# S5 on one core: the second family of outer products as swapped, negated copies

## The chip, the cores and the metric

The kernel runs on one core of a Trainium2 chip. The metric is the device time of one execution in microseconds; the median of several runs counts. Engines are named as in the profile: PE (TensorE), DVE (VectorE), ACT (ScalarE), POOL (GpSimd) and SP (the queue that issues DMAs). PEld is PE's loading of weights.

## What is computed

The kernel computes a whole network block and a second, two-layer one on 1024 tokens of width 1024, in float32. The change lies in one branch of the first block, the S5 state-space layer. It has 32 groups of 16 channels, and each group drives a complex diagonal state of 64 numbers:

```
bu_re = jnp.einsum('gpc,btgc->btgp', bbar_re, uf)
bu_im = jnp.einsum('gpc,btgc->btgp', bbar_im, uf)
_, _, x_re, x_im = lax.associative_scan(_complex_linear_combine, (a_re, a_im, bu_re, bu_im), axis=1)
y = (jnp.einsum('gcp,btgp->btgc', c_re.astype(f32), x_re)
     - jnp.einsum('gcp,btgp->btgc', c_im.astype(f32), x_im))
y = y.reshape(bsz, t, S5_WIDTH) + d_skip.astype(f32) * u.astype(f32)
```

Beside S5 stand a gated linear attention (GLA), an mLSTM, projections with gates and a feed-forward network; then the second block with a latent attention, a memory attention and a linear recurrence.

## The kernel before

Large matrix products are made of three matmuls each (`mm3`, L130): operands are split into a high and a low part (wh and wl of weights, ah and al of activations). Almost all work of DVE and POOL goes through small helpers, so a profile row names the helper's line: L136 is a two-operand operation, L145 a scalar-tensor-tensor, L142 a tensor-scalar, L148 an activation, L120 a matmul, L127 a transpose on PE.

S5 is done in chunks of 8 time steps, so that 1024 steps become 128 chunks. `s5_pre` (L636) makes tables once: E1 and E2 (powers of the diagonal state matrix times cosine and minus sine, in the lower 64 partitions a quarter turn further), the B and C matrices with sign, and the phases. `s5_core` (L734) runs eight times, for four groups each (hb 0 to 7); one such pass is called a round here. A round

- makes co and si, cosines and sines of the chunks' phases (x, y on DVE, two Sin activations and a square on ACT, `cossin` L725);
- makes outer products of B or C with powers (`prod`, L753): W1 on DVE; M1, M2 and W2 on POOL. M1 and W1 are one family; M2 and W2 are what they become when the state is multiplied by i. Each is a sum of two products, and each product is one instruction per group: 128x144 on DVE, 128x128 on POOL;
- transposes M1 and M2 on PE into a PSUM tile each and copies them to V1 and V2 with ACT (L772);
- multiplies the B columns (s_bst) with W1 into the kernel K of a chunk (L777 on), copies it with ACT (L779) and spreads it by eight DMAs into Tm (L783), to which DVE adds the skip weight on the diagonal (L785);
- loads the inputs U by eight DMAs, multiplies V1 and V2 with them into pa and pb (PSUM), turns those with co and si into va and vb, adds them, scans along the chunks (four scans, L808), and turns back into va and vb;
- adds Tm x U, W1 x va and W2 x vb in PSUM, and evicts that with a Gelu on ACT into ys, which a DMA stores.

va and vb share their buffers with x and y, so the next round's x waits until PE has read va.

The rounds are coroutines. Between them the main program goes on with large projections (four tiles `in_gqk`, one `in_misc`, then `in_v`, eight results of 24 matmuls each, evicted as e by ACT at L544). A planner mixes them: it keeps a clock (`self.clk`) that each matmul and transpose advances (L119, L126), and a coroutine that yields 14.0, 9.0 or 7.0 is resumed when the clock has gone on that far. Within what this emits, the framework's scheduler orders the instructions of each engine when the program is built; on the chip every engine works its queue in that fixed order. PSUM tiles for small results come from two rings, of three buffers and of one (`psc`, L233); every fourth call takes the second.

```
prod(W1, self.s5cr, self.s5E1, self.s5ci, self.s5E2, 0, 9, ALU.add, nc.vector, "tm")
prod(M1, self.s5br, self.s5E1, self.s5bi, self.s5E2, 9, 8, ALU.add, nc.gpsimd, "tmp")
prod(M2, self.s5bi, self.s5E1, self.s5br, self.s5E2, 9, 8, ALU.subtract, nc.gpsimd, "tmp")
prod(W2, self.s5cr, self.s5E2, self.s5ci, self.s5E1, 1, 8, ALU.subtract, nc.gpsimd, "tmp")
```

Of the kernel before, what the change touches and what calls it, by code (L numbers as in the profile page):

```python
# [10 lines left out]
F32 = mybir.dt.float32  # L11
# [3 lines left out]
AF = mybir.ActivationFunctionType  # L15
ALU = mybir.AluOpType
# [35 lines left out]
class Kernel:  # L52
# [681 lines left out]
    def s5_core(self, hb, pm, pu, pt, su, turn):  # L734

        nc = self.nc
        g0 = 4 * hb
        gs = slice(g0, g0 + 4)
        if hb:
            yield from self.join(turn[hb - 1])  # L740
        co = pm.tile([128, 4, 129], F32, tag="co", name="co")
        si = pm.tile([128, 4, 129], F32, tag="si", name="si")
        x = pt.tile([128, 4, 129], F32, tag="x", name="x")
        y = pt.tile([128, 4, 129], F32, tag="y", name="y")
        self.tt(x, self.s5ph[:, gs].unsqueeze(2).to_broadcast([128, 4, 129]),
                self.s5k[:, 17:146].unsqueeze(1).to_broadcast([128, 4, 129]), ALU.mult)
        self.cossin(co, si, x, y)
        W1 = pm.tile([128, 4, 9, 16], F32, tag="W1", name="W1")
        W2 = pm.tile([128, 4, 8, 16], F32, tag="W2", name="W2")
        M1 = pt.tile([128, 4, 8, 16], F32, tag="M1", name="M1")  # L750
        M2 = pt.tile([128, 4, 8, 16], F32, tag="M2", name="M2")

        def prod(out, m1, e1, m2, e2, a, n, op, eng, tag):  # L753
            tm = pt.tile([128, 4, 9, 16], F32, tag=tag, name="tm")
            for g in range(4):
                Eg = lambda e: e[:, g0 + g, a:a + n].unsqueeze(2).to_broadcast([128, n, 16])
                Cg = lambda m: m[:, g0 + g].unsqueeze(1).to_broadcast([128, n, 16])
                self.tt(tm[:, g, 0:n], Cg(m1), Eg(e1), ALU.mult, eng=eng)
                self.tt(out[:, g], Cg(m2), Eg(e2), ALU.mult, eng=eng)
            self.tt(out, tm[:, :, 0:n], out, op, eng=eng)  # L760
        prod(W1, self.s5cr, self.s5E1, self.s5ci, self.s5E2, 0, 9, ALU.add, nc.vector, "tm")
        prod(M1, self.s5br, self.s5E1, self.s5bi, self.s5E2, 9, 8, ALU.add, nc.gpsimd, "tmp")
        prod(M2, self.s5bi, self.s5E1, self.s5br, self.s5E2, 9, 8, ALU.subtract, nc.gpsimd, "tmp")
        prod(W2, self.s5cr, self.s5E2, self.s5ci, self.s5E1, 1, 8, ALU.subtract, nc.gpsimd, "tmp")
        yield 14.0
        V1 = pm.tile([128, 4, 128], F32, tag="V1", name="V1")
        V2 = pm.tile([128, 4, 128], F32, tag="V2", name="V2")
        for M, V in ((M1, V1), (M2, V2)):
            ps = self.psc()
            for g in range(4):  # L770
                self.tr(ps[:, g * 128:g * 128 + 128], M[:, g].rearrange("p a b -> p (a b)"))
            nc.scalar.copy(V, ps.rearrange("p (g n) -> p g n", g=4))  # L772
        self.finish(turn[hb])
        K = pt.tile([16, 4, 128], F32, tag="K", name="K")
        ps = self.psc()
        for g in range(4):
            self.mm(ps[0:16, g * 128:g * 128 + 128], self.s5bst[:, g0 + g],  # L777
                    W1[:, g, 0:8].rearrange("p a b -> p (a b)"), True, True)
        nc.scalar.copy(K, ps[0:16].rearrange("p (g n) -> p g n", g=4))  # L779
        Tm = pm.tile([128, 4, 128], F32, tag="Tm", name="Tm")  # L780
        nc.gpsimd.memset(Tm, 0.0)
        for j in range(8):
            nc.sync.dma_start(Tm[16 * j:16 * j + 16, :, 16 * j:128], K[:, :, 0:128 - 16 * j])  # L783
        for g in range(4):
            self.stt(Tm[:, g], self.ident, self.s5d[:, g0 + g:g0 + g + 1], Tm[:, g], ALU.mult, ALU.add)  # L785

        yield from self.join(su[hb // 2])
        U = pu.tile([128, 4, 128], F32, tag="U", name="U")
        src = self.d_u[hb // 2].rearrange("(g c) (j n) -> j c g n", g=8, j=8)
        for j in range(8):  # L790
            nc.sync.dma_start(U[16 * j:16 * j + 16], src[j][:, 4 * (hb % 2):4 * (hb % 2) + 4])
        Z = pu.tile([128, 4, 129], F32, tag="Z", name="Z")
        nc.gpsimd.memset(Z[:, :, 0:1], 0.0)
        yield 9.0
        va = pt.tile([128, 4, 128], F32, tag="x", name="va")
        vb = pt.tile([128, 4, 128], F32, tag="y", name="vb")
        pa, pb = self.psc(), self.psc()
        r4 = lambda a: a.rearrange("p (g n) -> p g n", g=4)
        for g in range(4):
            c = slice(g * 128, g * 128 + 128)  # L800
            self.mm(pa[:, c], V1[:, g], U[:, g], True, True)
            self.mm(pb[:, c], V2[:, g], U[:, g], True, True)
        self.tt(va, r4(pa), co[:, :, 1:129], ALU.mult)
        self.tt(vb, r4(pb), si[:, :, 1:129], ALU.mult)
        self.tt(va, va, vb, ALU.add)
        for g in range(4):
            R = self.s5R[:, g0 + g:g0 + g + 1].to_broadcast([128, 128])
            nc.vector.tensor_tensor_scan(out=Z[:, g, 1:129], data0=R, data1=va[:, g], initial=0.0,  # L808
                                         op0=ALU.mult, op1=ALU.add)
        self.tt(va, Z[:, :, 0:128], co[:, :, 0:128], ALU.mult)  # L810
        self.tt(vb, Z[:, :, 0:128], si[:, :, 0:128], ALU.mult)
        yield 7.0
        ys = pt.tile([128, 4, 128], F32, tag="ys", name="ys")
        ps = self.psc()
        for g in range(4):
            c = slice(g * 128, g * 128 + 128)
            self.mm(ps[:, c], Tm[:, g], U[:, g], True, False)
            self.mm(ps[:, c], W1[:, g, 1:9].rearrange("p a b -> p (a b)"), va[:, g], False, False)
            self.mm(ps[:, c], W2[:, g].rearrange("p a b -> p (a b)"), vb[:, g], False, True)
        self.act(ys, r4(ps), AF.Gelu_apprx_tanh)  # L820
        nc.sync.dma_start(self.d_sy[hb // 2][:, 512 * (hb % 2):512 * (hb % 2) + 512], ys.rearrange("p g n -> p (g n)"))
# [1071 lines left out]
    def mla_attn(self, d_mem):  # L1893

        nc, A = self.nc, self.A
        with ExitStack() as es:
# [164 lines left out]
            def take(gen, n):  # L2061
                for _ in range(n):
                    next(gen, None)
# [11 lines left out]
            M0 = (0, 0, 0, 0, 6, 1, 1, 1, 1, 0, 0, 0)  # L2075
            M1 = (0, 0, 0, 0, 0, 0, 1, 4, 2, 3, 4, 2)
            steps = []
# [6 lines left out]
            for n, (u, kb, first, last) in enumerate(steps):  # L2084
# [9 lines left out]
                take(mx[0], (M0[i] + 1) // 2)  # L2094
                take(mx[1], (M1[i] + 1) // 2)
                while len(pend) > 2 or (pend and n == len(steps) - 1):
# [9 lines left out]
                take(mx[0], M0[i] // 2)  # L2106
                take(mx[1], M1[i] // 2)
                take(pj, PJ[i])
# [379 lines left out]
```

## Time and profile before

| | us |
|---|---|
| median of 3 runs | 2833.54 (2833.21 to 2842.47) |
| the profiled execution | 2830.67 |
| its span, first to last instruction | 2828.9 |
| busy in the span: PE, DVE, ACT, POOL | 2681.6, 1719.8, 931.4, 858.8 |
| mean granted clock of PE | 0.978 of full speed |

The profile is of one execution. Busy time is the time in which an engine works on at least one instruction; matmuls overlap, so their starts tell their pace better than their durations. A window's row gives, for a stretch of the span, the busy time of each engine with its instructions, and the clock that PE was granted (1.00 is 2.4 GHz, 0.50 would be 1.2 GHz throughout). A wait's row says which operation stood idle until which other operation ended.

### The profile page before, as it was taken

How to read it: one execution, taken by the hardware profiler on the slowest of the kernel's cores; microseconds unless marked ns; L12 is line 12 of the kernel's file. 1: busy time of each engine (PE TensorE's matmuls, PEld its weight loads, DVE VectorE, ACT ScalarE, POOL GpSimd, SP SyncE). 2: the span in 40 equal slices, each digit the busy share in tenths (PEclk: the TensorE clock that was granted, in tenths of full speed). 3: DMA queues.
4: the chain of work that ended last, by engine and by line, in shares of the span. 5: the costliest groups of instructions: out<-in, count | busy, mean ns of one | idle time of the engine just before them, and what ended most of it. 6: DMA issues, size and time to landing. Idle time of an engine off the chain costs nothing. (4 is left out here: it accounts for less than half of the span.)

```text
span 2828.9 us, 40596 instructions
## 1 busy us (share of the span) xinstructions
PE 2681.6 (95%) x16104; PEld 2210.0 (78%) x16104; DVE 1719.8 (61%) x2467; ACT 931.4 (33%) x1431; POOL 858.8 (30%) x771
## 2 busy tenths in 40 slices
PE   6989899899999999799999999999989998999998
PEld 5769688688878899689898888787766665976688
DVE  7896975662643245944444466653577777667586
ACT  6453544311111133422222321242333434146330
POOL 4694561000000003744444200141213547013332
PEclk8999999999999999899999999999999999999999
DMA  8323224552645242222222423342220113322231
GB/s 245 109 74 111 98 79 139 171 185 98 234 176 168 75 164 97 76 86 79 90 71 86 149 90 103 107 144 90 81 82 29 34 44 106 141 82 61 74 110 62
DMA packets 133917, 304.13 MB, mean 108 GB/s; under 512 B 18032, under 2 KB 61888, under 8 KB 133600
## 3 DMA queue, kind: packets, MB, share of 16 engines
q1 hardware_dynamic: 133728, 301.54, 31.6%
q8 instruction: 127, 2.08, 0.3%
q14 instruction: 62, 0.51, 0.1%
HBM read 226.20 MB, written 73.94 MB: 106 GB/s over the span
## 5 line engine op out<-in xcount | busy, mean ns | idle before, releaser
L120 PE MATMUL psg<-ah,wh 128*128 128x512 f32 x1392 | 560.4, 404 | 11.4 <-ACT ah L424 7.5
L120 PE MATMUL psg<-ah,wl 128*128 128x512 f32 x1392 | 554.8, 399 | 3.0 <-DVE wl L136 3.0
L120 PE MATMUL psg<-al,wh 128*128 128x512 f32 x1392 | 553.7, 398 | 1.8 <-DVE al L136 1.7
L136 DVE TENSOR_TENSOR wl<-wr,wh 128x1024 fp32r<-128x1024 f32 (+3 forms) x212 | 274.3, 1296 | 374.2 <-ACT wh L179 252.4
L179 ACT CAST wh<-wr 128x1024 fp32r<-128x1024 f32 (+3 forms) x161 | 162.3, 1010 | 775.5 <-PE psg L120 352.8
L120 PEld LDWEIGHTS psg<-ah,wh 128*128 128x128 f32 x1392 | 263.6, 190 | 79.2 <-issue 11.0
L120 PEld LDWEIGHTS psg<-al,wh 128*128 128x128 f32 x1392 | 264.5, 190 | 65.7 <-issue 5.3
L120 PEld LDWEIGHTS psg<-ah,wl 128*128 128x128 f32 x1392 | 264.3, 190 | 64.4 <-DVE wl L136 3.9
L120 PE MATMUL psc<-wh,ah 128*128 128x256 f32 x1024 | 290.5, 284 | 8.4 <-DVE ystore L136 4.3
L120 PE MATMUL psc<-wl,ah 128*128 128x256 f32 x1024 | 287.2, 281 | 0.0
L120 PE MATMUL psc<-wh,al 128*128 128x256 f32 x1024 | 286.5, 281 | 0.0
L142 POOL TENSOR_SCALAR rsv<-ss 128x1 f32<-128x1 f32 x32 | 11.3, 354 | 754.0 <-DVE ss L1249 512.1
L120 PEld LDWEIGHTS psc<-wh,ah 128*128 128x128 f32 x1024 | 196.6, 192 | 13.3 <-DVE ystore L136 5.0
L120 PE MATMUL psc<-tx,wh 128*128 128x256 f32 x1088 | 195.1, 280 | 2.6 <-DVE e L136 2.6
L120 PEld LDWEIGHTS psc<-wl,ah 128*128 128x128 f32 x1024 | 195.8, 191 | 0.3
L120 PEld LDWEIGHTS psc<-wh,al 128*128 128x128 f32 x1024 | 195.4, 191 | 0.1
L136 POOL TENSOR_TENSOR e<-e 128x1024 f32<-128x1024 f32 (+3 forms) x65 | 109.4, 1687 | 242.7 <-ACT e L148 122.9
L120 PEld LDWEIGHTS psc<-tx,wh 128*128 128x128 f32 x1088 | 169.3, 188 | 6.0 <-issue 2.8
L136 POOL TENSOR_TENSOR acc<-acc,e 128x512 f32<-128x512 f32 (+2 forms) x60 | 116.2, 1937 | 158.9 <-PE psc L120 156.5
L136 DVE TENSOR_TENSOR e<-psc,e 128x512 f32<-128x512 f32 (+1 forms) x138 | 89.8, 666 | 106.5 <-PE psc L120 106.4
L120 PE MATMUL psc<-tx,wl 128*128 128x256 f32 x544 | 152.1, 280 | 0.0
L120 PE MATMUL psc<-wh,gh 128*128 128x512 f32 x352 | 139.1, 397 | 2.4 <-ACT gh L1470 2.4
(488 smaller groups left out, 5454.4 us busy)
## 6 DMA issues: line engine op xcount, KB each, us to landing
wr<-in_w_ws_dram SPq DMA_DIRECT2D x45, 512.0 KB
wr<-in_ffn_in_dram SPq DMA_DIRECT2D x44, 512.0 KB
aw<-in_ada_w_dram SPq DMA_DIRECT2D x32, 512.0 KB
wr<-in_w_out_dram SPq DMA_DIRECT2D x24, 512.0 KB
d_h<-e SPq DMA_DIRECT2D x22, 512.0 KB
wr<-in_ffn_out_dram SPq DMA_DIRECT2D x22, 512.0 KB
e<-d_h SPq DMA_DIRECT2D x22, 512.0 KB
e<-d_y SPq DMA_DIRECT2D x20, 512.0 KB
```

The costliest lines, as they stand in the source:

```text
L120: self.nc.tensor.matmul(out, lhsT, rhs, start=start, stop=stop)
L136: (eng or self.nc.vector).tensor_tensor(out=out, in0=a, in1=b, op=op)
L142: (eng or self.nc.vector).tensor_scalar(out=out, in0=a, scalar1=s1, scalar2=s2, op0=op0, op1=op1)
L179: (self.nc.vector.tensor_copy if self.hi_dve else self.nc.scalar.copy)(hi[:, :n], raw[:, :n])
```

## The change

The families are no longer computed twice. Because the lower 64 partitions of E1 and E2 are a quarter turn ahead, the second family is the first with its halves of 64 swapped, one of them negated. W2 is made by two ACT copies from W1, one of each half, the second with scale -1. M2 is not made at all: M (formerly M1) is transposed once, and V2 comes from the same PSUM tile as V1, by two ACT copies of 64 columns per group each. The products that remain (W1 on DVE, M on POOL) run over four groups in one instruction.

```diff
@@ -747,29 +747,32 @@
         W1 = pm.tile([128, 4, 9, 16], F32, tag="W1", name="W1")
         W2 = pm.tile([128, 4, 8, 16], F32, tag="W2", name="W2")
-        M1 = pt.tile([128, 4, 8, 16], F32, tag="M1", name="M1")
-        M2 = pt.tile([128, 4, 8, 16], F32, tag="M2", name="M2")
-
-        def prod(out, m1, e1, m2, e2, a, n, op, eng, tag):
-            tm = pt.tile([128, 4, 9, 16], F32, tag=tag, name="tm")
-            for g in range(4):
-                Eg = lambda e: e[:, g0 + g, a:a + n].unsqueeze(2).to_broadcast([128, n, 16])
-                Cg = lambda m: m[:, g0 + g].unsqueeze(1).to_broadcast([128, n, 16])
-                self.tt(tm[:, g, 0:n], Cg(m1), Eg(e1), ALU.mult, eng=eng)
-                self.tt(out[:, g], Cg(m2), Eg(e2), ALU.mult, eng=eng)
-            self.tt(out, tm[:, :, 0:n], out, op, eng=eng)
-        prod(W1, self.s5cr, self.s5E1, self.s5ci, self.s5E2, 0, 9, ALU.add, nc.vector, "tm")
-        prod(M1, self.s5br, self.s5E1, self.s5bi, self.s5E2, 9, 8, ALU.add, nc.gpsimd, "tmp")
-        prod(M2, self.s5bi, self.s5E1, self.s5br, self.s5E2, 9, 8, ALU.subtract, nc.gpsimd, "tmp")
-        prod(W2, self.s5cr, self.s5E2, self.s5ci, self.s5E1, 1, 8, ALU.subtract, nc.gpsimd, "tmp")
+        M = pt.tile([128, 4, 8, 16], F32, tag="M", name="M")
+
+        def prod(out, m1, m2, a, n, eng, tag):
+
+            tm = pt.tile([128, 4, 9, 16], F32, tag=tag, name="tm")[:, :, 0:n]
+            Eg = lambda e: e[:, gs, a:a + n].unsqueeze(3).to_broadcast([128, 4, n, 16])
+            Cg = lambda m: m[:, gs].unsqueeze(2).to_broadcast([128, 4, n, 16])
+            self.tt(tm, Cg(m1), Eg(self.s5E1), ALU.mult, eng=eng)
+            self.tt(out, Cg(m2), Eg(self.s5E2), ALU.mult, eng=eng)
+            self.tt(out, tm, out, ALU.add, eng=eng)
+        prod(W1, self.s5cr, self.s5ci, 0, 9, nc.vector, "tm")
+        prod(M, self.s5br, self.s5bi, 9, 8, nc.gpsimd, "tmp")
+
+        top, bot = slice(0, 64), slice(64, 128)
+        nc.scalar.copy(W2[top], W1[bot, :, 1:9])
+        self.act(W2[bot], W1[top, :, 1:9], AF.Copy, scale=-1.0)
         yield 14.0
         V1 = pm.tile([128, 4, 128], F32, tag="V1", name="V1")
         V2 = pm.tile([128, 4, 128], F32, tag="V2", name="V2")
-        for M, V in ((M1, V1), (M2, V2)):
-            ps = self.psc()
-            for g in range(4):
-                self.tr(ps[:, g * 128:g * 128 + 128], M[:, g].rearrange("p a b -> p (a b)"))
-            nc.scalar.copy(V, ps.rearrange("p (g n) -> p g n", g=4))
+        ps = self.psc()
+        for g in range(4):
+            self.tr(ps[:, g * 128:g * 128 + 128], M[:, g].rearrange("p a b -> p (a b)"))
+        pv = ps.rearrange("p (g n) -> p g n", g=4)
+        nc.scalar.copy(V1, pv)
+        nc.scalar.copy(V2[:, :, top], pv[:, :, bot])
+        self.act(V2[:, :, bot], pv[:, :, top], AF.Copy, scale=-1.0)
         self.finish(turn[hb])
```

A round calls `psc` five times instead of six, and the planner's clock gets four transposes less a round, so the queues of S5 are ordered anew; behind S5 only the first GLA steps stand otherwise than before. On PE, the distance between a round's products with U and its output products is 30 to 35 large matmuls in the rounds 2 to 4, as before; the transposes and the product for K of the next round lie in it, after 12 of them. In the rounds beside `in_v`, three results of 24 lie in it instead of two.

POOL's queue before, one round of four groups (W_ and M_ with numbers are that round's W2, M1 and M2):

```order
L136 TENSOR_TENSOR M_1675<-s_bi,s_E_866 128x128 x4
L136 TENSOR_TENSOR tm<-s_br,s_E_865 128x128 x4
L136 TENSOR_TENSOR M_1676<-s_br,s_E_866 128x128 x4
L793 MEMSET Z 128x4
L136 TENSOR_TENSOR M_1675<-tm,M_1675 128x512
L136 TENSOR_TENSOR tm<-s_bi,s_E_865 128x128 x4
L136 TENSOR_TENSOR M_1676<-tm,M_1676 128x512
L781 MEMSET Tm 128x512
L136 TENSOR_TENSOR W_1674<-s_m,s_E_865 128x128 x4
L136 TENSOR_TENSOR tm<-s_m,s_E_866 128x128 x4
L136 TENSOR_TENSOR W_1674<-tm,W_1674 128x512
```

and in the changed program:

```order
L796 MEMSET Z 128x4
L136 TENSOR_TENSOR tm<-s_br,s_E_865 128x4x128
L784 MEMSET Tm 128x512
L136 TENSOR_TENSOR M<-s_bi,s_E_866 128x512
L136 TENSOR_TENSOR M<-tm,M 128x512
```

Of 24 products and three sums, two products and one sum are left.

ACT's queue before, from one output of S5 (ys) to the next table load for an output (V_1616 and V_1617 are a round's V1 and V2):

```order
L148 ACTIVATE ys<-psc 128x512
L148 ACT_TABLE_LOAD
L148 ACTIVATE si<-x 128x516
L148 ACTIVATE co<-x 128x516
L148 ACTIVATE co<-co 128x516
L772 COPY V_1616<-psc 128x512
L772 COPY V_1617<-psc 128x512
L179 CAST wh<-wr 128x1024
L601 COPY e<-psg 128x1024
L779 COPY K<-psc 16x512
L148 ACT_TABLE_LOAD
```

and the same stretch now (W_1373 is W2, W_1372 is W1):

```order
L148 ACTIVATE ys<-psc 128x512
L764 COPY W_1373<-W_1372 64x512
L148 ACTIVATE W_1373<-W_1372 64x512
L148 ACT_TABLE_LOAD
L148 ACTIVATE si<-x 128x516
L148 ACTIVATE co<-x 128x516
L148 ACTIVATE co<-co 128x516
L773 COPY V_1480<-psc 128x512
L774 COPY V_1481<-psc 128x4x64
L148 ACTIVATE V_1481<-psc 128x4x64
L782 COPY K<-psc 16x512
```

The two W2 copies have come between ys and the table load for the sines, and V2 is two instructions.

DVE's queue now, from a round's x on (W_1533 is W1; before, the products with tm and W stood as four of 128x144, and the additions to Tm among those with tm):

```order
L136 TENSOR_TENSOR x<-s_ph,s_kr 128x516
L136 TENSOR_TENSOR W_1533<-s_m,s_E_866 128x576
L145 SCALAR_TENSOR_TENSOR Tm<-ident,s_d,Tm 128x128 x4
L142 TENSOR_SCALAR y<-x 128x516
L136 TENSOR_TENSOR W_1533<-tm,W_1533 128x576
L136 TENSOR_TENSOR x<-x,y 128x516
L136 TENSOR_TENSOR tm<-s_m,s_E_865 128x576
L136 TENSOR_TENSOR vb<-psc,si 128x512
L136 TENSOR_TENSOR va<-psc,co 128x512
L142 TENSOR_SCALAR co<-co 128x516
L136 TENSOR_TENSOR va<-va,vb 128x512
```

The additions to Tm have moved ahead in the round; in the first round they stand just before the last row shown, in the third before the first.

## Rows read from the trace of the kernel before

**Rows 1.** The page, part 1: busy us, share of the span, instructions.

```profile
PE 2681.6 (95%) x16104; PEld 2210.0 (78%) x16104; DVE 1719.8 (61%) x2467; ACT 931.4 (33%) x1431; POOL 858.8 (30%) x771
```

**Rows 2.** Windows: PE, PEld, DVE, ACT, POOL busy, PEclk, DMA share, GB/s.

```profile
110.00:150.00 40.00, 34.72 (x197) 27.45 (x196) 32.49 (x50) 17.75 (x25) 39.37 (x65) 1.00 0.27 87
150.00:190.00 40.00, 35.27 (x201) 29.23 (x202) 34.95 (x57) 16.90 (x22) 39.29 (x66) 0.96 0.26 77
190.00:230.00 40.00, 34.15 (x238) 30.49 (x237) 38.87 (x65) 20.26 (x27) 34.80 (x54) 0.87 0.29 95
230.00:280.00 50.00, 49.83 (x398) 47.10 (x397) 27.81 (x48) 18.39 (x29) 17.69 (x29) 0.97 0.31 93
```

**Rows 3.** Waits of PE, 110 to 235 us: total us, times, longest.

```profile
PE psc L120 <- DVE va L136: 4.5, 3, 2.2
PE psc L120 <- ACT V L772: 3.2, 1, 3.2
PE psc L127 <- ACT e L544: 2.0, 1, 2.0
PE psc L127 <- DVE va L136: 2.0, 2, 1.8
PE psc L120 <- ACT e L544: 2.0, 1, 2.0
```

**Rows 4.** Window of one round of S5, columns as in rows 2.

```profile
155.83:173.87 18.04, 16.54 (x99) 13.34 (x98) 16.94 (x27) 8.46 (x11) 17.80 (x29) 1.00 0.18 60
```

**Rows 5.** Tile tm and its readers: ns min/median/max, first and last start, forms.

```profile
L136 POOL TENSOR_TENSOR tm<-s_br,s_E x32: 399/461/1265, 98.9 to 224.9; 128x128 f32<-128x128 f32 x32
L136 DVE TENSOR_TENSOR tm<-s_m,s_E x32: 293/504/520, 99.3 to 228.1; 128x144 f32<-128x144 f32 x32
...
L136 DVE TENSOR_TENSOR W<-tm,W x8: 746/951/1742, 105.9 to 245.1; 128x576 f32<-128x576 f32 x8
L136 POOL TENSOR_TENSOR W<-tm,W x8: 1267/1285/2372, 117.9 to 243.7; 128x512 f32<-128x512 f32 x8
```

**Rows 6.** Timeline of DVE, POOL busy beside it and later idle: start, duration.

```profile
167.08 0.89 DVE L136 TENSOR_TENSOR va<-va,vb 128x512 f32<-128x512 f32 x1
168.00 1.94 DVE L808 TENSOR_TENSOR_SCAN Z<-s_R,va 128x128 f32<-128x128 f32 x4
...
250.26 0.69 DVE L136 TENSOR_TENSOR va<-va,vb 128x512 f32<-128x512 f32 x1
250.99 1.37 DVE L808 TENSOR_TENSOR_SCAN Z<-s_R,va 128x128 f32<-128x128 f32 x4
```

**Rows 7.** Timeline of PE: transposes of M1 and M2 together, and of one.

```profile
180.98 1.03 PE L127 MATMUL psc<-ident,M 128*128 128x128 f32 x8
...
203.84 0.60 PE L127 MATMUL psc<-ident,M 128*128 128x128 f32 x4
```

**Rows 8.** Groups of ACT, 76 to 285 us: count, busy us, mean ns, idle before.

```profile
L148 ACT ACT_TABLE_LOAD x19 | 24.4, 1283 | 4.4 <-DMA cum<-d_gc 4.1
...
L772 ACT COPY V<-psc 128x512 f32<-128x512 f32 x16 | 8.9, 582 | 4.9 <-PE psc L127 4.8
L544 ACT COPY e<-psc 128x256 f32<-128x256 f32 x16 | 5.8, 369 | 25.4 <-PE psc L120 25.4
```

**Rows 9.** Timeline of PE: two large matmuls in a row at full clock.

```profile
284.59 0.39 PE L120 MATMUL psg<-ah,wh 128*128 128x512 f32 x1
284.82 0.39 PE L120 MATMUL psg<-al,wh 128*128 128x512 f32 x1
```

**Rows 10.** Timeline: K's copy on ACT, and DVE's addition to that Tm.

```profile
251.42 0.58 ACT L779 COPY K<-psc 16x512 f32<-16x512 f32 x1 [0.39 <-PE psc L120]
...
259.27 1.14 DVE L145 SCALAR_TENSOR_TENSOR Tm<-ident,s_d,Tm 128x128 f32<-128x128 f32 x4 [5.59 <-DMA Tm<-K]
```

**Rows 11.** Timeline of DVE: x and tm of a round with POOL mostly idle.

```profile
223.83 0.83 DVE L136 TENSOR_TENSOR x<-s_ph,s_kr 128x516 f32<-128x516 f32 x1
...
227.48 0.95 DVE L136 TENSOR_TENSOR tm<-s_m,s_E 128x144 f32<-128x144 f32 x4
```

## The prediction

> **What bounds the kernel now.** The page's busy shares come first: PE is busy 95% of the span and DVE 61%, POOL 30% [rows 1], so a gain has to come out of PE's own work, out of the 5% in which it stands still, or out of stretches at the lower clock. Then the stages: S5 lies between about 100 and 280 us, and its windows show all three at once [rows 2]. In 110 to 230 PE is idle for 5.28 + 4.73 + 5.85 = 15.9 us (the next 50 us add 0.17). In the same 120 us POOL is busy 39.37, 39.29 and 34.80 of every 40 and DVE 32.5 to 38.9; after 230, when POOL's S5 work runs out, PE is full. The granted clock is 1.00, 0.96, 0.87 and 0.97 of full speed; shares below 1 are time at 1.2 instead of 2.4 GHz behind such idle stretches, and cost about 0.04 x 35.3 + 0.13 x 34.2 + 0.03 x 49.8 = 7.3 us of PE.
>
> Who ends PE's idle time stands in the waits of 110 to 235 [rows 3]: mostly va, DVE's last link, as operand or as the reader that frees a PSUM tile, then the V copies on ACT (once, at the start), and ACT's e copies (twice 2.0 us). So the stage is set by DVE with POOL beside it. A round of four groups, from one start of x to the next, is 18.04 us long [rows 4]; POOL is busy 17.8 of it, DVE 16.9, PE 16.5, ACT 8.5. Two engines are full, and the third waits a little for them.
>
> **What the change removes.** POOL: of a round's 24 outer products of 128x128 and three sums of 128x512, two products and one sum of 128x512 are left. The sum alone takes 1.27 us at least, 1.29 in the median [rows 5]; a product over four groups is at least that long and at most four small ones, 4 x 0.46 = 1.84. So POOL's S5 arithmetic falls from some 17 us a round to 3.8 to 5.0.
>
> DVE: eight products of 128x144 become two of 128x576. The small ones take 0.29 us at best and 0.50 in the median, the sum of 576 elements 0.75 and 0.95 [rows 5]; 8 x 0.50 = 4.0 against 2 x 0.95 = 1.9, or 2.3 against 1.5 without contention. I take 1.5 us a round.
>
> DVE's other instructions get shorter as well, because POOL leaves. The same add takes 0.89 us beside POOL and 0.69 without it, the four scans 1.94 and 1.37 [rows 6]. That is about a quarter of what they cost; on 16.9 us of DVE less the 1.5 just counted, that is some 3 to 4 us where POOL is away. DVE's round falls to about 11 to 12 us of work against PE's 16. It is then no longer full, and neither is POOL.
>
> PE: four of eight transposes a round go. Four take 0.60 us by themselves and eight 1.03 [rows 7], so four cost 0.43 and eight rounds 3.4 us. This is PE's own work and comes off the end whatever else happens.
>
> **What it adds.** ACT gets the two W2 copies of 64x512, and V2 as two halves of 128x256 where one copy of 128x512 stood. The nearest rows are 0.58 for a 128x512 copy and 0.37 for 128x256 [rows 8]; K's copy of 16x512 takes 0.58 [rows 10], so elements per partition count, and partitions don't. No row shows a copy that moves half the partitions to the other half: between 0.37, if half the volume were half the work, and the 1.28 of a table load, the dearest small thing on ACT, I take 0.6, by the two rows of 512 elements. The far end would add 1.4 us of latency a round. That makes 2 x 0.6 + 2 x 0.37 - 0.58 = 1.4 us a round, on an engine busy 8.5 of 18. As load it is free. As latency it is not: by the order the copies stand between ys and the next table load (1.28 us), so that load, done early before, now follows the W2 copies, which follow DVE's W1. Behind them wait si, co, the V copies and, in the last rounds, the e copies that free PE's PSUM tiles. Counted from the end of a round's output products, DVE makes x, y, W1 and x in 2.9 us (3.65 from x to tm in a round without POOL, less 0.7 for the four small products that become one) [rows 11], the W2 copies end at 3.5, the load at 4.8, si and both co steps at 6.6. DVE meets co in its queue between the products va, vb and their sum, which it reaches at about 5.8 (12 large matmuls and the eight products with U come first on PE). It waits 1 us there and ends va and vb at 10.2 to 11.2. PE needs va after 12 + 12 + 18 large matmuls at 0.23 us [rows 9] and some 3.1 us of small ones, at about 12.7. The cover is 1.5 to 2.5 us; it holds, and were it gone each microsecond would cost one per round.
>
> The order moves one more thing. The diagonal addition to Tm is now queued on DVE ahead of that sum in the first round, and at the head of the round in the third. Tm is ready 7.3 us after the copy of K ends [rows 10]. In the first round that puts va some 1 to 2 us after PE's arrival; in the third it delays x by under 2 us, inside the cover. The eight DMAs a round that carry K into Tm, the loads of U and the weight loads are the same in number.
>
> **The sum**, against the profiled execution's 2830.67 us (2.9 under the median of the three runs, 2833.54). Transposes: -3.4. Idle: of 15.9 us, the waits on DVE and V go; the two waits on ACT's e copies (4.0) need not, since they come in the long cumulative sums of the gate, and 1 us in the first round is new. I count -11. Clock: idle that goes takes its slow stretch with it, in proportion 11 / 15.9 of 7.3, rounded down to -4 because the deepest stretch, 0.87, is the one with the e copies. Outside S5 the two programs are ordered alike but for the early GLA steps, where rows change places within a few microseconds: 0, within -3 and +3. Together -18.4. On the median that is 2815.1, on the profiled execution 2812.3; I say **2814**. Its own range: at best every idle and slow microsecond comes back, 3.4 + 15.9 + 7.3 = 26.6, which is 2804 on the profiled execution.
>
> **Rival 1: latency instead of load.** PE's waits were those of one chain per round (co, va, vb, scan, va, vb), and the chain keeps its length: DVE's instructions get shorter, but the W2 copies and the exposed table load on ACT and the wait for Tm's DMA in DVE's queue put back what that saved. For it: ACT was idle half the round and yet PE waited once for its V copies. Against it: in rows 6 the chain shrinks by a fifth as soon as POOL stops, and from 230 on PE had no wait. PE then gains the transposes, the start-up wait of 3.2 and 1 to 2 us of clock, 8 us: 2825. From where: if the chain ends 2 us later than I add it up.
>
> **Rival 2, slower: the long POOL instruction shuts DVE out.** Four short instructions become one of 1.3 us or more, and M waits for the transposes, so POOL starts its block just when DVE is on the chain's sum, scans and products. If each of the three made DVE wait out its whole length, at worst the 2.3 us of the longest 512-element row [rows 5], the chain would grow by 6.9 us. Less 3 us for the cover and the shorter instructions, that is 3.9 us of idle a round, 31 in eight, where 16 are now; the slow clock would double with it. That gives +15 + 7 - 3.4 = +19, about 2852. It decides from 5 us a round on. Against it: sums of 512 elements already stand three times a round on POOL, and DVE beside them was lengthened by 0.2 us in the median of its own sum (0.75 to 0.95) and by 1.0 at most [rows 5]. The Trainium skill's "SBUF — State Buffer", section "Who interferes with whom", has the rule that speaks for it: a DVE instruction with two SBUF inputs and a POOL instruction that reads SBUF contend for a port pair that is locked for the whole instruction, and the later one blocks fully. By that rule in its strict form the 6.9 us hold and the time is rival 2's. The trace agrees that the two contend, but its 0.2 us beside a POOL sum of 1.29 us is far from a full block.
>
> That the work is not really removed is no rival: the order lists the two products and the sum on POOL, and four transposes.
>
> **Chances.** Forecast 0.66; rival 1 0.27; rival 2 0.05; another slow-down, in the reordered GLA steps, 0.02. About 0.5%, or 14 us, is what a measurement of this kernel can tell from no change, so "faster" means below 2819.4: the forecast and its best bound lie there. Rival 1 lies within 0.5%, rival 2 and the rest above. So 0.66, 0.27, 0.07. The range goes from the best bound, 2804, to rival 1 with the 3 us of the GLA steps, 2828.
>
> **What would show it.** Right: from 110 us on POOL busy under 8 us in 20 and PE's idle under 6 us up to the end of S5, rounds of 16 to 16.5 us, the scans of a round near 1.4 us, 32 transposes of M instead of 64, the last S5 output near 258 instead of 277 us, GLA as long as before. Rival 1: DVE idle on co or on Tm's DMA in each round, and PE waiting for va by 1 us or more. Rival 2: DVE products of 1.5 us and more beside POOL's. Wrong altogether: S5 ends 15 us or more earlier, and the stages behind it give that back.

## The result, and the profile after

The changed kernel takes 2812.11 us (median of 5 runs, 2806.06 to 2820.0), the kernel before 2833.54 (5 runs, 2829.37 to 2842.47): a ratio of 0.9921, 95% interval 0.9895 to 0.9948. The profiled execution of the changed kernel took 2806.06 us with a span of 2804.2; it is the fastest of the five, so its positions are compared with those of the profiled execution before, stage by stage, and not the two spans.

Page, part 1 (against [rows 1]), then the windows of S5 (against [rows 2]; columns as there). POOL has lost 100 us, DVE 32.5; PE's share is the same 95% of a shorter span.

```profile
PE 2671.5 (95%) x16072; PEld 2203.3 (79%) x16072; DVE 1687.3 (60%) x2419; ACT 940.9 (34%) x1455; POOL 758.6 (27%) x579
```

```profile
110.00:150.00 40.00, 38.94 (x224) 32.18 (x223) 27.66 (x52) 22.62 (x36) 9.23 (x11) 1.00 0.36 111
150.00:190.00 40.00, 40.00 (x235) 33.40 (x235) 31.21 (x51) 28.43 (x39) 9.04 (x10) 0.96 0.30 94
190.00:230.00 40.00, 37.34 (x301) 35.83 (x300) 30.55 (x58) 23.71 (x37) 9.87 (x10) 0.91 0.35 107
```

PE is idle for 1.06, 0 and 2.66 us of the three windows, where it was 5.28, 4.73 and 5.85; POOL went from 39, 39 and 35 of 40 to between 9 and 10. From one start of x to the next (131.73, 147.78, 161.84) two rounds take 16.1 and 14.1 us instead of 18.04 [rows 4]. The groups of ys, the output of a round, give the end of S5: its last start moves from 277.1 to 255.9 us. First the kernel before, then the changed one (ns min/median/max, first and last start).

```profile
L148 ACT ACTIVATE ys<-psc x8: 597/599/602, 135.3 to 277.1; 128x512 f32<-128x512 f32 x8
```

```profile
L148 ACT ACTIVATE ys<-psc x8: 597/598/600, 129.7 to 255.9; 128x512 f32<-128x512 f32 x8
```

The waits of PE from 100 to 300 us (against [rows 3]) have none left for va of S5 and none for e on ACT; the 2.7 for vb is one wait near 208 us, the 0.8 for V is S5's start, and the three others lie behind 262 us, at the beginning of GLA. One wait of 0.3 for W at the start is not shown.

```profile
PE psc L120 <- DVE e L145: 4.7, 1, 4.7
PE psc L120 <- DVE vb L136: 2.7, 1, 2.7
PE psc L120 <- ACT P L954: 2.3, 1, 2.3
PE psc L120 <- DVE mx L136: 2.1, 1, 2.1
PE psc L120 <- ACT V L773: 0.8, 1, 0.8
```

GLA then gives a part back. The windows go from 100 us to GLA's first d, on to its last Sz, and over both; first before, then changed.

```profile
100.00:281.70 181.70, 165.67 (x1082) 143.90 (x1081) 144.09 (x236) 75.65 (x105) 141.16 (x231) 0.95 0.29 91
281.70:428.60 146.90, 128.64 (x2314) 111.13 (x2313) 120.09 (x198) 71.82 (x171) 85.77 (x91) 0.93 0.26 92
100.00:428.60 328.60, 294.31 (x3394) 255.02 (x3393) 264.18 (x434) 147.47 (x276) 226.92 (x322) 0.94 0.28 91
```

```profile
100.00:260.10 160.10, 156.04 (x1043) 137.77 (x1042) 111.79 (x190) 86.60 (x131) 39.38 (x40) 0.97 0.33 103
260.10:410.10 150.00, 133.44 (x2321) 115.18 (x2320) 121.12 (x197) 71.82 (x171) 86.69 (x91) 0.89 0.26 90
100.00:410.10 310.10, 289.48 (x3362) 252.95 (x3361) 232.91 (x386) 158.42 (x301) 126.07 (x131) 0.93 0.29 97
```

Up to GLA 21.6 us are gained. GLA takes 3.1 longer for almost the same number of matmuls: its PE idle falls by 1.7 us, its PE time rises by 4.8 at a granted clock of 0.89 instead of 0.93. Over both, 18.5 us are gained, 13.7 of idle (34.3 to 20.6) and 4.8 of PE's busy time.

One thing stands in the new trace that the old one hid. The timelines of POOL and DVE from 99 us on, where POOL starts on M; the changed kernel:

```profile
99.06 1.48 POOL L136 TENSOR_TENSOR tm<-s_br,s_E 128x512 f32<-128x512 f32 x1 [19.89 <-DVE s_E L136]
100.50 1.58 POOL L136 TENSOR_TENSOR M<-s_bi,s_E 128x512 f32<-128x512 f32 x1
...
99.53 1.62 DVE L136 TENSOR_TENSOR tm<-s_m,s_E 128x576 f32<-128x576 f32 x1
101.07 1.56 DVE L136 TENSOR_TENSOR x<-s_ph,s_kr 128x516 f32<-128x516 f32 x1
```

and the kernel before, at the same place:

```profile
100.94 3.42 POOL L136 TENSOR_TENSOR W<-s_m,s_E 128x128 f32<-128x128 f32 x7
...
101.06 0.89 DVE L136 TENSOR_TENSOR x<-s_ph,s_kr 128x516 f32<-128x516 f32 x1
```

The same x of 516 elements takes 0.69 us alone (its median in the changed kernel, in ns below), 0.89 beside POOL products of 128 elements and 1.56 beside one of 512; POOL's product, 1.06 alone, takes 1.48 to 1.58. Neither overlaps much with the other: DVE's tm ends 0.61 us after POOL's tm (it takes 0.75 alone), POOL's M ends 0.93 after that, and x 0.55 after M. They take turns, instruction by instruction. This is the turn theory of the later runs.

```profile
L136 DVE TENSOR_TENSOR x<-s_ph,s_kr x8: 664/690/1558, 101.1 to 223.6; 128x516 f32<-128x516 f32 x8
```

### The profile page after: what moved, and what is told of

Same layout as the page of the kernel before. It is cut to its first block, busy times and chain, and to the rows that moved or that the text cites. A ratio compares the mean times of both kernels' runs of the same rounds, so it can differ in the third digit from the quotient of the medians.

```text
span 2804.2 us, 40321 instructions
## 1 busy us (share of the span) xinstructions
PE 2671.5 (95%) x16072; PEld 2203.3 (79%) x16072; DVE 1687.3 (60%) x2419; ACT 940.9 (34%) x1455; POOL 758.6 (27%) x579
## 5 line engine op out<-in xcount | busy, mean ns | idle before, releaser
L120 PE MATMUL psc<-tx,wh 128*128 128x256 f32 x1088 | 188.4, 277 | 2.6 <-DVE e L136 2.6
```

Source lines behind the costliest of these rows:

```text
L120: self.nc.tensor.matmul(out, lhsT, rhs, start=start, stop=stop)
```

## The experiments

Of each run the table has the start of the first and the last output of S5 in its profiled execution, and the time against the kernel before with its 95% interval; each ratio is taken against runs of the kernel before of the same batch, so it is not the quotient of two medians of the table. A kernel's own runs lie up to 23 us apart (tr_back: 2807.36 to 2830.11), so the outputs, although of one execution each, are the finer measure for S5, and the ratio is the only one for the whole.

| run | first ys | last ys | median us | ratio |
|---|---|---|---|---|
| before | 135.3 | 277.1 | 2833.54 | 1 |
| changed | 129.7 | 255.9 | 2812.11 | 0.9921 (0.9895 to 0.9948) |
| merge_only | 141.1 | 282.1 | 2843.31 | 1.0045 (1.0030 to 1.0060) |
| copies_only | 129.9 | 257.7 | 2810.93 | 0.9927 (0.9912 to 0.9942) |
| w2_pool | 138.2 | 268.8 | 2832.23 | 0.9995 (0.9983 to 1.0006) |
| v2_pool | 137.2 | 275.0 | 2833.25 | 1.0010 (0.9998 to 1.0023) |
| dve_merge | 137.3 | 277.9 | 2835.86 | 1.0016 (1.0002 to 1.0030) |
| pool_merge | 144.4 | 287.0 | 2841.69 | 1.0032 (1.0020 to 1.0045) |
| tr_back | 130.1 | 258.4 | 2814.02 | 0.9930 (0.9911 to 0.9949) |
| rotate_sum | 130.0 | 261.5 | 2807.85 | 0.9911 (0.9897 to 0.9925) |
| pool_load | 133.7 | 263.7 | 2818.55 | 0.9943 (0.9926 to 0.9960) |
| pool_load_small | 131.3 | 260.5 | 2818.95 | 0.9946 (0.9924 to 0.9967) |
| mix | 127.9 | 255.2 | 2807.76 | 0.9901 (0.9878 to 0.9925) |
| rot_diag | 127.9 | 253.2 | 2811.40 | 0.9922 (0.9899 to 0.9944) |

### The change taken apart: merging, W2, V2

**merge_only**: the loop over groups goes, the four families and eight transposes stay.

```diff
-            for g in range(4):
-                self.tt(tm[:, g, 0:n], Cg(m1), Eg(e1), ALU.mult, eng=eng)
-                self.tt(out[:, g], Cg(m2), Eg(e2), ALU.mult, eng=eng)
+            self.tt(tm, Cg(m1), Eg(e1), ALU.mult, eng=eng)
+            self.tt(out, Cg(m2), Eg(e2), ALU.mult, eng=eng)
```

> The kernel before with its four families of products (W1 on DVE; M1, M2, W2 on POOL), each run over four groups at once; eight transposes a round, no swapped copies. Load theory (PE waited because POOL and DVE were both full): POOL does three blocks of about 1.06 + 1.47 + 1.38 = 3.9 us a round, 11.7 instead of 17.8, and so is no longer full, but DVE stays contended for 70% of a round. Most of PE's idle goes, the transposes (3.4 us) stay: the last S5 output at 262 to 268 us (277 before, 256 after), the time 2817 to 2825. Merging is all: everything but the transposes comes back, last output near 259, 2815. Port lock (a long POOL instruction shuts DVE out): DVE instructions beside POOL double, 70% of the time, the chain gets longer; last output at 275 or later, 2832 or more.

**copies_only**: the changed kernel with that loop put back into its two families.

> The changed kernel with its two remaining families cut back into products per group (8 small products and a sum on POOL, the same on DVE, a round); the swapped copies stay. Load theory: POOL does some 8 x 0.46 + 1.3 = 5.0 us a round instead of 3.9, DVE 1 to 1.5 us more, neither near a round of 16; last S5 output at 256 to 259 us, the time within 3 us of the changed kernel. Merging is all: the gain falls back to the transposes and little else, last output at 268 or later, 2822 or more. Port lock: DVE no longer meets POOL instructions of over 1.3 us except one sum a round, so its doubled instructions go; last output at 255 or earlier, and the early GLA steps no worse.

**w2_pool**: the changed kernel with

```diff
-        nc.scalar.copy(W2[top], W1[bot, :, 1:9])
-        self.act(W2[bot], W1[top, :, 1:9], AF.Copy, scale=-1.0)
+        prod(W2, self.s5cr, self.s5E2, self.s5ci, self.s5E1, 1, 8, ALU.subtract, nc.gpsimd, "tmp")
```

> The changed kernel with W2 made by products on POOL again (two products and a sum over four groups) in place of ACT's two copies; V2 by copies, four transposes a round. Load theory: POOL 7.8 us a round, ACT 1.24 us less; PE does not wait for either, so the last S5 output lies at 256 to 260 us, the time 2812 to 2816. Latency theory (ACT's W2 copies ahead of the table load cost what the load frees): without them the chain is shorter and the last output earlier than 255.

**v2_pool**: the changed kernel with M2's products on POOL and its own transposes in place of V2's two half copies.

> The changed kernel with M2 made by products on POOL again (two products and a sum over four groups) and transposed, eight transposes a round, V2 by one copy from its own PSUM tile; W2 by ACT's copies. Load theory: as the changed kernel but for the transposes, 0.43 us a round, 3.4 in all, and a little contention from 3.9 us more POOL: last S5 output at 259 to 263 us, the time 2815 to 2819. If the transposes are hidden (PE has slack of its own in each round), the last output stays at 256 to 257.

The swapped copies carry the gain: copies_only, with its products cut back into groups, has a ratio of 0.9927 and its last output at 257.7 us, the whole change 0.9921 and 255.9. Merging alone costs 0.45%, some 13 us, of which 5 stand at the last output of S5. With only half of the copies, one family (W2 or M2) being still on POOL, the time is that of the kernel before. Both half-way kernels run their products over four groups and so pay for merging too; one with products per group was not run. The load theory expected them at 256 to 263 and missed by 9 and 12 us; for merge_only the port lock was right, for copies_only the load theory. The first window of merge_only, w2_pool and v2_pool, in this order, shows where the largest part is lost:

```profile
110.00:150.00 40.00, 29.30 (x161) 24.11 (x159) 34.58 (x32) 13.53 (x19) 32.69 (x26) 0.87 0.23 73
```

```profile
110.00:150.00 40.00, 30.29 (x156) 25.16 (x155) 29.82 (x37) 15.48 (x25) 20.00 (x17) 0.88 0.23 73
```

```profile
110.00:150.00 40.00, 33.24 (x173) 27.01 (x171) 33.59 (x42) 21.92 (x33) 21.67 (x17) 0.87 0.25 75
```

PE is idle for 10.7, 9.7 and 6.8 us there, of 19.5, 15.7 and 16.1 up to 230 us. POOL computes M and the rest of two rounds ahead without a pause, and until that is done every DVE instruction, down to the scalar step on y (0.42 us alone), takes about the length of a POOL instruction or more. In w2_pool:

```profile
105.48 1.52 DVE L142 TENSOR_SCALAR y<-x 128x516 f32<-128x516 f32 x1
106.92 1.62 DVE L136 TENSOR_TENSOR W<-tm,W 128x576 f32<-128x576 f32 x1
108.46 1.76 DVE L136 TENSOR_TENSOR x<-x,y 128x516 f32<-128x516 f32 x1
```

Going from merge_only's 282.1, removing W2 takes off 7.1, removing M2 with its transposes 13.3, and both 26.2.

### Turns at SBUF: which engine's length matters

**dve_merge** and **pool_merge**: the kernel before, with only DVE's or only POOL's families over four groups.

```diff
+            if eng is nc.vector:
+                self.tt(tm[:, :, 0:n], Cg(m1), Eg(e1), ALU.mult, eng=eng)
+                self.tt(out, Cg(m2), Eg(e2), ALU.mult, eng=eng)
-            for g in range(4):
+            for g in range(0 if eng is nc.vector else 4):
```

(pool_merge has `nc.gpsimd` in both places.)

> The kernel before with the W1 family of DVE alone run over four groups at once (two products of 128x576 in place of eight of 128x144); POOL's three families stay in products per group. Turn theory (DVE and POOL take turns at SBUF instruction by instruction, each waits out the other's current one): a DVE instruction of 576 elements meets one POOL product of 0.46 us and takes 0.95 to 1.0, so W1 costs 3.0 instead of 4.7 us a round; POOL's instructions do not get shorter, POOL stays busy over 90% of 110 to 230. The last S5 output comes at 268 to 275 us (277 before, 282 with all four merged), the time 2820 to 2832. Length theory (merging itself is what cost merge_only its 5 us, whichever engine it is on): later than 277.

> The kernel before with POOL's three families run over four groups at once, and DVE's W1 family left in products per group. Turn theory: each of DVE's small products (0.29 us alone) waits out a POOL instruction of 1.1 to 1.4 us, so beside POOL they take about 1.1 us each, 8 to 9 us a round for W1's eight products where POOL is busy, against 4.0 before; this is the worst of all: last S5 output at 283 to 295 us, the time 2840 to 2855. Load theory (fewer, longer instructions save POOL time and nothing else): POOL falls from 17 to 12 us a round, last output at 270 to 277, the time 2822 to 2832.

pool_merge came as the turn theory has it, the latest of all. Beside POOL's long instructions DVE's first four products of 128x144 take 4.45 us, 1.11 each where 0.29 is their time alone; the next eight 0.72 each, two to a turn of POOL:

```profile
99.21 4.45 DVE L136 TENSOR_TENSOR tm<-s_m,s_E 128x144 f32<-128x144 f32 x4
...
105.07 5.78 DVE L136 TENSOR_TENSOR W<-s_m,s_E 128x144 f32<-128x144 f32 x8
```

dve_merge missed its range, by 2.9 us at the last output. That 277.9 lies in the range of the length theory does not make that right: DVE did get its 0.95 us an instruction. But POOL stayed full, 39.37 of 40 us and more up to 230, and now PE waited for POOL's M itself:

```profile
PE psc L127 <- POOL M L136: 9.6, 6, 3.5
```

DVE's longer instructions hold POOL up in turn. The same first 15 products of POOL take 12.7 us from their first start (99.54) instead of 7.3 (from 98.87); their last four, in the kernel before and in dve_merge:

```profile
104.32 1.87 POOL L136 TENSOR_TENSOR M<-s_bi,s_E 128x128 f32<-128x128 f32 x4
```

```profile
108.59 3.63 POOL L136 TENSOR_TENSOR M<-s_bi,s_E 128x128 f32<-128x128 f32 x4
```

So DVE relieved alone changes nothing, because POOL's volume stays and its turns get longer. The reverse is not true: copies_only relieves POOL, leaves DVE its eight products a round, and has nearly the whole gain. What set a round of the kernel before was POOL's work, its own time together with what it cost DVE.

**pool_load**: the changed kernel computes M a second time, into a tile X that nobody reads. **pool_load_small**: the same, X in products per group. **mix**: no X; M in products per group, W1 over four groups.

```diff
         prod(M, self.s5br, self.s5bi, 9, 8, nc.gpsimd, "tmp")
+        X = pt.tile([128, 4, 8, 16], F32, tag="X", name="X")
+        prod(X, self.s5br, self.s5bi, 9, 8, nc.gpsimd, "tmp")
```

> The changed kernel, and behind M's family on POOL the same two products and sum over four groups once more, into a tile that nobody reads: 3.9 us more POOL a round, 7.8 in all, with no new wait on PE or ACT. Turn theory: POOL and DVE exclude each other at SBUF for the length of an instruction, so the load alone lengthens DVE's queue: while POOL runs ahead, up to about 118 us, every DVE instruction takes 1.5 us or more, the first S5 output comes at 135 to 138 us (129.7 in the changed kernel, 138.2 with W2 on POOL) and the last at 262 to 268. Product theory (the two half-way kernels were late because PE waited for the products themselves, M2 and W2): an unread block costs nothing, first output at 129.5 to 131, last at 256 to 258.

> As the run before, but the unread family is computed in products per group (eight of 128x128 and one sum over four groups, some 5 us of POOL a round); M and W1 stay over four groups. Turn theory: a DVE instruction meets turns of 0.46 us instead of 1.1 to 1.5, so less is lost although POOL's volume is the same and its time longer: first S5 output at 131 to 134 us, last at 258 to 263, earlier than with the long instructions. Volume theory (only the elements that POOL moves count): within 1 us of the run before.

> The changed kernel with M on POOL in products per group, and W1 on DVE over four groups. Turn theory: DVE's instructions of 99 to 111 us, 1.5 to 1.6 us each beside POOL's long ones, take 0.9 to 1.0, and the wait of PE for V at the start (0.8 us) goes; PE is the bound behind that, so the last S5 output comes at 253.5 to 256 us, the time 2809 to 2813. If the length of POOL's instructions did not matter: DVE stays at 1.5 us there.

An unread block of 3.9 us a round moves the last output by 7.8 us, which excludes the product theory's 256 to 258, and the same work in short instructions moves it by 4.6 only. The first output of pool_load, 133.7, comes earlier than the turn theory's 135 to 138. In the time of the whole neither load is clear of noise against the changed kernel: the intervals overlap.

This contention does not explain all of the half-way kernels: of w2_pool's 12.9 us over the changed kernel 5 are left, of v2_pool's 19.1 some 9 beside the transposes (below). PE's longest waits in them are for V, 7.4 and 4.7 us, but not because M came late. In w2_pool M was transposed at 108.02; V's copy, 13 us later, stands on ACT behind the next round's si and co, which wait for x on DVE (PE, then ACT):

```profile
108.02 0.60 PE L127 MATMUL psc<-ident,M 128*128 128x128 f32 x4
...
120.59 0.63 ACT L148 ACTIVATE si<-x 128x516 f32<-128x516 f32 x1 [6.80 <-DVE x L136]
...
121.66 0.57 ACT L770 COPY V<-psc 128x512 f32<-128x512 f32 x1
```

In the changed kernel and in pool_load V's copies stand ahead of that si (at 114.42 and 116.28); in v2_pool, with M transposed at 106.91, V1's copy comes at 116.45 and V2's, behind that si, at 122.02. So in the half-way kernels ACT's queue is in another order, and by it an x that is late on DVE holds PE up. No run changed that order alone, so how much of the 5 and 9 us it makes up stays open.

In mix, DVE's first instructions fall to 0.96 and 0.89 and the wait for V goes, as expected:

```profile
99.42 0.96 DVE L136 TENSOR_TENSOR tm<-s_m,s_E 128x576 f32<-128x576 f32 x1
100.31 0.89 DVE L136 TENSOR_TENSOR x<-s_ph,s_kr 128x516 f32<-128x516 f32 x1
```

The first output comes 1.8 us earlier than in the changed kernel, the last 0.7. Its time is the lowest median, 2807.76, just under the range expected, but its interval and the changed kernel's overlap.

### The transposes, and less work for PE

**tr_back**: the changed kernel with a second PSUM tile.

```diff
         nc.scalar.copy(V1, pv)
+        ps = self.psc()
+        for g in range(4):
+            self.tr(ps[:, g * 128:g * 128 + 128], M[:, g].rearrange("p a b -> p (a b)"))
+        pv = ps.rearrange("p (g n) -> p g n", g=4)
```

> The changed kernel with four transposes of M a round added into a second PSUM tile, from which V2's two halves are copied. If the transposes are PE's own work on the path: 0.43 us a round, the last S5 output 3 to 4 us later than the changed kernel's 255.9, that is 259 to 260, the time 2814 to 2817. If they are hidden: 256 to 257. If the second PSUM tile makes PE wait for a free one: over 261.

The 32 transposes move the last output by 2.5 us, between the two ranges expected and nearer to the first: they are mostly PE's own work on the path, a little less than the 3.4 counted.

**rotate_sum** exchanges halves of vectors instead of matrices, so that V2, W2 and their products go:

```diff
-            self.mm(pb[:, c], V2[:, g], U[:, g], True, True)
...
-        self.tt(vb, r4(pb), si[:, :, 1:129], ALU.mult)
+        self.tt(vb[top], r4(pa)[bot], si[bot, :, 1:129], ALU.mult)
+        self.stt(vb[bot], r4(pa)[top], -1.0, si[top, :, 1:129], ALU.mult, ALU.mult)
...
-        self.tt(vb, Z[:, :, 0:128], si[:, :, 0:128], ALU.mult)
+        self.stt(vb[top], Z[bot, :, 0:128], -1.0, si[bot, :, 0:128], ALU.mult, ALU.mult)
+        self.tt(vb[bot], Z[top, :, 0:128], si[top, :, 0:128], ALU.mult)
+        self.tt(va, va, vb, ALU.add)
...
-            self.mm(ps[:, c], W2[:, g].rearrange("p a b -> p (a b)"), vb[:, g], False, True)
```

> The changed kernel without W2 and V2: since W2 and V2 are W1 and V1 with their halves exchanged and one negated, the exchange is made on vectors instead: vb = si times the other half of pa (two half products on DVE, one negated), and behind the scan va + exchanged vb, added on DVE, goes through W1 alone. PE loses 8 of 20 large-S5 products a round: 8.0 of 16.1 us with V and 12.7 us with W, 20.8 in all by the changed kernel's rows, ACT the two W2 copies and two half copies, 2.0 us a round; DVE gains two half products and a sum, 2.1 us a round on some 12.5. If PE still sets the round (14.0 us at best 13.4): last S5 output at 236 to 240 us, the time 2792 to 2796. If DVE's chain sets it (14.6 us a round and waits for Tm's DMA): 244 to 252, the time 2798 to 2808. If GLA gives it back: no faster than 2806.

**rot_diag** adds to it, beside M in products per group as in mix (dI is the identity times d, made once):

```diff
-        yield 14.0
+        yield 12.5
...
+        self.tt(K[:, :, 0:16], K[:, :, 0:16], self.s5dI[:, gs], ALU.add, eng=nc.gpsimd)
-        for g in range(4):
-            self.stt(Tm[:, g], self.ident, self.s5d[:, g0 + g:g0 + g + 1], Tm[:, g], ALU.mult, ALU.add)
...
-        yield 7.0
+        yield 8.5
```

> The version with exchanged vectors (rotate_sum), with three more edits: the diagonal of Tm is added to the 16x16 blocks of K on POOL before the DMAs (32 additions of 128x128 leave DVE, 9.1 us, with their waits for Tm's DMA, 6.3), M on POOL in products per group, and the planner's pauses set to 12.5 and 8.5 instead of 14 and 7, for a round of about 14 us. DVE falls from some 14.6 to 13.3 us a round. If DVE's queue is what held rotate_sum: S5 and the first GLA steps end 6 to 12 us earlier, the time 2796 to 2803. If PE's work in front of GLA only moves, and GLA's own chain sets the end of the stage: 2803 to 2809.

Neither is clearly faster than the changed kernel. rotate_sum's last output, 261.5, comes 5.6 us later than the changed kernel's and after both ranges, 236 to 240 and 244 to 252; its time, 2807.85, fits the case that GLA gives the gain back and that of DVE's chain. rot_diag's last output comes 8.3 us earlier than rotate_sum's, but GLA does not start earlier, and its time, 2811.40, lies above both of its ranges. The windows up to GLA's first d and from there to its last Sz, rotate_sum and then rot_diag:

```profile
100.00:258.90 158.90, 152.26 (x962) 132.44 (x961) 134.29 (x217) 73.97 (x99) 42.06 (x39) 0.97 0.34 107
258.90:409.40 150.50, 124.95 (x2270) 107.76 (x2269) 107.59 (x193) 70.33 (x170) 86.43 (x91) 0.88 0.25 84
```

```profile
100.00:259.30 159.30, 145.64 (x936) 127.07 (x935) 118.31 (x182) 73.05 (x100) 58.96 (x96) 0.95 0.34 107
259.30:409.90 150.60, 128.93 (x2299) 112.49 (x2298) 115.60 (x197) 70.90 (x170) 88.97 (x91) 0.86 0.25 85
```

PE's busy time over both windows falls from 289.5 to 277.2 and 274.6 us, and its idle time rises from 20.6 to 32.2 and 35.3. Work was taken off PE, and the stage did not get shorter: GLA starts at 259 us and lasts 150, as in the changed kernel (260 and 150). In front of GLA, PE's longest waits are now for W1 of DVE, in rot_diag 11.6 us at once, from 182.5 us on: the shorter pause brings the product of K to PE before DVE has made W1, and DVE spends 9.4 us of that stretch on the gate's cumulative sums and their input (gla, e):

```profile
PE psc L120 <- DVE W L136: 12.6, 2, 11.6
```

What the first d of GLA waits for is the same DMA in all three, here in the changed kernel:

```profile
260.08 0.69 DVE L136 TENSOR_TENSOR d<-cum 128x512 f32<-128x512 f32 x1 [4.37 <-DMA cum<-d_gc]
```

SP issues it at 255.49 us in the changed kernel, at 254.78 in rotate_sum and at 254.16 in rot_diag, behind a store of e and loads of weights in its queue. Moving it was not tried, nor what holds GLA's length.

## Why the prediction was right, and which steps were not

The time, 2812.11 against 2814, lies in the range, and the mechanism is the one forecast: POOL is relieved, and with it DVE. That the number is so close is partly luck, as the steps show:

- **POOL and DVE no longer full**: right. POOL's products over four groups take 1.06 to 1.47 us and its sum 1.38 in the median, 3.9 us a round against 3.8 to 5.0; W1's products on DVE fall from 29.9 to 15.9 us in eight rounds, a saving of 1.75 a round against 1.5. copies_only and pool_load show that POOL's relief is on the path. DVE's 1.5 us a round are hardly on it: copies_only has eight products a round again and ends S5 only 1.8 us later. "The stage is set by DVE with POOL beside it" gives DVE too much; relieved alone, in dve_merge, it brings nothing.
- **Transposes, -3.4**: right in kind, 2.5 by tr_back.
- **ACT's added copies, cover 1.5 to 2.5 us**: right. W2's copies take 0.62 and 0.63 us (0.6 taken), DVE's product va waits for co four times, 6.2 us in all, and the additions for Tm's DMA five times, 13.8 in all, which is the first sign named for rival 1; but PE never waits for va: of all that one wait of 2.7 us reaches it, for vb, which stands behind Tm's additions in DVE's queue. The two kinds, of DVE from 100 to 260 us (total, times, longest):

```profile
DVE Tm L145 <- DMA Tm<-K: 13.8, 5, 4.6
...
DVE va L136 <- ACT co L148: 6.2, 4, 1.9
```

- **Idle, -11**: too small. The two waits on ACT's e, "need not" go, are gone, and the 1 us that was to be new in the first round did not come; in S5 16.0 us became about 4, and with GLA -13.7.
- **Clock, -4**: too large. Busy time fell by 4.8 us over S5 and GLA, of which the transposes are 2.5 to 3.4; that leaves 1.4 to 2.3. For S5 alone it was about right: reckoned as in the prediction, 0.05 of 165.67 us became 0.03 of 156.04, some 3.6 less. GLA gave part of it back.
- **GLA as long as before**: wrong by 3.1 us, just outside the 3 allowed. S5's end came 2 us earlier than the 258 forecast, so the errors of the steps cancel: -18.5 at the end of GLA, against a sum of -18.4. That is luck. Another 6.2 us lie behind GLA in the two profiled executions, and no term stands for them.
- **Rival 2's mechanism was dismissed on a wrong reading.** The step is "its 0.2 us beside a POOL sum of 1.29 us is far from a full block". The median of 0.95 us there came from meeting POOL's short products, the other kind of instruction in its queue, and 0.2 us is what waiting out one of those costs. The one of its eight that came in behind a POOL sum of 512 elements was blocked for 1.0 us (1.74 less 0.75); in the kernel before:

```profile
109.13 1.36 POOL L136 TENSOR_TENSOR M<-tm,M 128x512 f32<-128x512 f32 x1
...
109.37 1.74 DVE L136 TENSOR_TENSOR W<-tm,W 128x576 f32<-128x576 f32 x1
```

In the changed kernel the block beside a POOL product of 512 elements is 0.87 us (1.56 less 0.69) of a POOL time of 1.06, and the sign named for rival 2, DVE products of 1.5 us and more, does show. The Trainium skill's "SBUF — State Buffer", section "Who interferes with whom", has it that a DVE instruction with two SBUF inputs contends with a POOL one that reads SBUF, and one with at most one SBUF input, outside the two-port modes, does not. The trace agrees: the product of PSUM and co, with one SBUF input, takes 675 to 692 ns in all eight rounds, in four of them with POOL at work beside it, while x and the scans double where they meet POOL. The scalar step on y, whose one input lies in SBUF, is lengthened too (0.42 to 1.52, in w2_pool); the same section of the Trainium skill counts that operation among those that can use both ports. The rival itself fell all the same: POOL is busy for 9 of 40 us, behind the start few DVE instructions meet it (four scans at 170.78 took 3.25 us instead of 1.37, timelines of DVE and POOL below), and none of it reaches PE as a wait for va. With POOL busy 24 to 33 of 40 us, in merge_only and pool_merge, the rival's slow-down is what happens, though smaller: 0.45% and 0.32%, where 19 us would be 0.67%.

```profile
170.78 3.25 DVE L811 TENSOR_TENSOR_SCAN Z<-s_R,va 128x128 f32<-128x128 f32 x4
...
171.00 1.06 POOL L136 TENSOR_TENSOR M<-s_bi,s_E 128x512 f32<-128x512 f32 x1 [8.83 <-PE psc L127]
172.13 1.30 POOL L136 TENSOR_TENSOR M<-tm,M 128x512 f32<-128x512 f32 x1
```

The sum also hid that its terms don't add: the prediction priced POOL's relief as one piece, and either half of it alone, with long products, is worth nothing in time.

## What to carry to other kernels

Where DVE and POOL run side by side on SBUF operands, ask how long the other engine's single instruction is, not only how busy it is: merging POOL's and DVE's short instructions into long ones made this kernel 0.45% slower, although POOL's busy time fell. With most of POOL's work gone the length hardly mattered (copies_only against the changed kernel). Taking work off one of two engines that contend can show nothing, as in dve_merge, where taking it off the other shows nearly everything, as in copies_only; and parts of a change that show nothing singly, as w2_pool and v2_pool, can be worth it together. And a microsecond won on the busiest engine, PE's 12 us in rotate_sum, is worth only what the next stage's start lets through.

## What was not expected of the hardware

DVE and POOL taking turns nearly whole instructions long (x of 516 elements 0.69, 0.89 and 1.56 us) was not expected at this size. Nor was this: the same 2678 matmuls of a later stage, which the change does not touch, took 5.5 us less in one profiled execution than in the other, at almost the same granted clock. First before, then changed:

```profile
1153.60:1609.67 456.07, 435.58 (x2678) 390.79 (x2679) 233.03 (x274) 137.92 (x176) 203.62 (x118) 0.98 0.25 87
```

```profile
1135.50:1586.03 450.53, 429.61 (x2678) 384.98 (x2679) 231.66 (x275) 138.01 (x177) 204.65 (x118) 0.97 0.25 89
```

That is part of why the two spans differ by 24.7 us where 18.5 were gained up to the end of GLA, and such stretches may be why runs of one kernel lie up to 23 us apart. What sets the pace there stays open.
